# Hybrid decoder step on one core: another VectorE order while h is made, and norm2 written in place

## The chip, the core and the metric

The kernel runs on one core of a Trainium2 chip. A core has five engines that run their own instruction streams and meet through semaphores: TensorE (PE) multiplies matrices, VectorE (DVE) and ScalarE (ACT) do elementwise work, GpSimd (POOL) and SyncE (SP) issue transfers here. The metric is the time of one execution on the device in microseconds, the median of several.

## The reference, cut to what matters

One layer of a decoder trunk over 1056 tokens (1024 of a prompt, 32 of samples: 8 requests of 4) with 1024 features:

```python
mod = (silu(c) @ w_ada + b_ada).reshape(bsz, 6, D_MODEL)      # shift1, scale1, gate1, shift2, scale2, gate2
h = rmsnorm(x, norm1_g) * (1 + scale1) + shift1
u_ssm, u_pool, g_ssm, g_pool = split(h @ w_in)                # 1024 -> 3072
y_ssm = s5_mixer(u_ssm, ...)                                  # diagonal complex state space model
merged = sigmoid(g_ssm) * glu(gelu(y_ssm)) + sigmoid(g_pool) * pool_mixer(u_pool, ...)
x = x + gate1 * (merged @ w_out)
h2 = rmsnorm(x, norm2_g) * (1 + scale2) + shift2
f_a, f_b = split(h2 @ w_ffn_in)
x = x + gate2 * ((silu(f_a) * f_b) @ w_ffn_out)
y = rmsnorm(x, normf_g)
```

The modulations differ between the prompt and each sample request. All inputs and outputs are float32.

## The kernel before

**Tiles.** Activations lie with features on the 128 partitions and tokens along the row: X[k], k = 0 to 7, is a tile of 128 features by 1056 tokens. Tokens go in three column groups G0 = 0 to 384, G1 = 384 to 768, G2 = 768 to 1056; the last 32 columns are the samples. Every float32 operand is kept as a high and a low part, and each product is three matmuls: high by high (L510), low activation by high weight (L511), high activation by low weight (L512). For an activation the high part is written by ACT and the low part by DVE; `split` (L484) makes the parts of a weight, `whi` on ACT (L488) and `wlo` on DVE (L489), in a ring of four buffers each.

**The start.** The sums of squares of x run through PE (L685), DVE takes the reciprocal root (`rsqrt`, L563 to L573), PE broadcasts it with four `pick` matmuls, and ACT copies them to R (L710, L711). In between come the modulations of feature tiles 0 and 1: `ada_main(m, hq)` multiplies w_ada on PE (L609) and copies the result with ACT to `adat` (L695); `ada_fin` turns it with two small matmuls (L616) and writes mod[m] on DVE (L619, L621, L623), m = 1 for the scale and m = 0 for the shift. hq counts pairs of feature tiles, so hq = 0 to 3.

**The h stage.** For each feature tile, `h_scale` scales x in place on DVE (L641, and three small operations for the samples, L598 to L600) and has ACT add the shift into `hh` (L644); `h_lo` makes `hl` on DVE from x, the shift and `hh` (L648). The first two column tiles of w_in, f = 0 and 1, are accumulated while the feature tiles appear: `gemm(kt, f)` multiplies feature tile kt. Between gemm(kt, 0) and gemm(kt, 1) of kt = 0, 2, 4 stand the modulations of the next pair.

**The S5 preparation.** The coefficients of the state space model are worked out by small DVE operations that are recorded first and written out later by `fill(n)`, n of them at a time (all have line L93); `fill(1000)` at the end of the h stage writes those that are left. Then S5 makes the matrices `wbr` and `wbi` (L125 to L131), which PE transposes into `tp` (L265), between pieces of the column tiles f = 2 and f = 3, each over all eight feature tiles.

**Norm 2 and the FFN.** After w_out, `residual` (L944) adds to X in place, and `norm2(g)` makes h2 for a column group: it scales X into a tile `xn` (L979), ACT and DVE make the high and low parts, and POOL stores `xn` to `hd` in HBM, and after the last group X to `xr` (L989). For the first FFN steps `ffn_in` (L1030) runs on h2; then `sums` loads pieces of `hd` back (`bq`, by SP, L1051), forms sums of them on DVE (`bf`, L1056 to L1059), and splits these (`th` on ACT, L1066; `tl` on DVE, L1067) for `product` (L1108), which runs the other FFN steps with fewer products of blocks (L1114 to L1116).

**What sets the order.** PE and SP keep the order in which the program is written, to the end. DVE and ACT keep it as long as `order` is open, which is until the column tile f = 3 is done; behind that a scheduler orders them by what is ready.

Of the kernel before, what the change touches and what calls it, by code (L numbers as in the profile page):

```python
# [10 lines left out]
F32 = mybir.dt.float32  # L11
# [16 lines left out]
NTOK = 1056  # L28
# [424 lines left out]
def trunk(ctx: ExitStack, tc: tile.TileContext, A, O):  # L453
    nc = tc.nc
# [37 lines left out]
    def split2(src):  # L492
        raw = load(src)
        return [split(raw[:, i]) for i in range(2)]

    def ahead(srcs):

        nxt = split2(srcs[0])
        for i in range(len(srcs)):
            cur, nxt = nxt, split2(srcs[i + 1]) if i + 1 < len(srcs) else None  # L500
            yield cur
# [132 lines left out]
    s5c = third.enter_context(pool("s5c"))  # L634
    s5 = S5(tc, s5c, psum, dram, ident, A["s5"], yd, O["pst"], O["sst"])

    wgen = ahead([A["w_in"][i] for i in (*range(2, 16), 22, 23, *range(16, 22))] + [A["w_glu"][i] for i in range(8)] + [A["w_out"][0]])

    def h_scale(kt, a=0, b=NTOK):
        x, e = X[kt], min(b, ST)  # L640
        v.scalar_tensor_tensor(x[:, a:e], x[:, a:e], mod[1][:, kt, 0:1], R[:, a:e], op0=MUL, op1=MUL)  # L641
        if b > ST:
            modulate_samples(x[:, ST:], R[:, ST:], mod[1], mod[0], kt, x[:, ST:])
        act.activation(hx(kt)[0][:, a:b], x[:, a:b], AF.Identity, bias=mod[0][:, kt, 0:1], scale=1.0)  # L644

    def h_lo(kt, a=0, b=NTOK):
# [5 lines left out]
    with ExitStack() as early:  # L652
        ring = early.enter_context(pool("ada"))
        s5t = early.enter_context(pool("s5t"))
        raw = {}

        def fetch(hq):
            for m in (1, 0):
                raw[m, hq] = [load(A["w_ada"][m, hq, pg], ring) for pg in range(2)]

        fetch(0)
        us_raw = [load(A["w_in"][f]) for f in range(2)]
        fetch(1)
        fetch(2)
        v.tensor_reduce(r32, ident.rearrange("p (q t) -> p t q", q=4), axis=mybir.AxisListType.X, op=ADD)
        prep = s5.prep(s5t)
        next(prep)
        for _ in prep:
            pass
        fill = s5.later.emit  # L670
        fetch(3)
        sq = (page("sq"), page("R1"))
        R = sq[1]
        ss = mm((128, 264))
        for k in range(8):
            q = sq[k % 2]
            for h in range(2):
                qh, xh = (z[:, 528 * h:528 * h + 528] for z in (q, X[k]))
                if h and k in (3, 5, 7):
                    v.tensor_mul(qh, xh, xh)  # L680
                    fill(5)
                else:
                    act.activation(qh, xh, AF.Square)
                for r in (2 * h, 2 * h + 1):
                    pe.matmul(ss[32 * r:32 * r + 32, :], ones[:, 0:32], q[:, 264 * r:264 * r + 264], start=k == 0,  # L685
                              stop=k == 7, tile_position=(0, 32 * r))
        act.activation(prm[:, 0:256], prm[:, 0:256], AF.Silu)
# [12 lines left out]

        x, y, t = (tmp()[:, 0:264] for _ in range(3))
        rsqrt(ss, x, y, t)
        ada_main(1, 0)
        ada_main(0, 0)
        ada_fin(0)
        fill(4)
        us_w = [[split(us_raw[f][:, 0])] for f in range(2)]
        for r in range(4):
            ps = mm((128, 264))
            pe.matmul(ps, pick[:, r, :], y, start=True, stop=True)  # L710
            act.copy(R[:, 264 * r:264 * r + 264], ps)  # L711
        us_ps = [[mmg(g) for g in range(3)] for f in range(2)]

        def gemm(kt, f):
            for g in range(3):
                feat(us_ps[f][g], w8(us_w[f]), hx, g, [kt], kt == 0, kt == 7)

        def ada_pair(hq):
            for m in (1, 0):
                ada_main(m, hq)  # L720

        h_scale(0, *GROUPS[0])
        h_scale(0, *GROUPS[1])
        h_lo(0, *GROUPS[0])
        h_scale(0, *GROUPS[2])
        h_lo(0, *GROUPS[1])
        h_scale(1)
        h_lo(0, *GROUPS[2])
        for kt in range(8):
            gemm(kt, 0)  # L730
            if kt < 6 and kt % 2 == 0:
                ada_pair(kt // 2 + 1)
            gemm(kt, 1)
            if kt < 6:
                if kt % 2 == 0:
                    ada_fin(kt // 2 + 1)
                h_scale(kt + 2)
            if kt < 7:
                h_lo(kt + 1)
            if kt == 1:  # L740
# [6 lines left out]
    s5.pool = s5p  # L747
    pump = Pump(s5.run())

    w_next = next(wgen)  # L750
    for f in range(4):
        if f >= 2:
            w = w_next if f == 2 else next(wgen)
        if f == 2:
            pumps.append(pump)
        for g in range(3):
            if f < 2:
                ps = us_ps[f][g]
# [201 lines left out]
    acc, R = page("acc2"), page("R2")  # L960
    mx = h2x = hx
    xr = dram.tile([8, 128, NTOK], F32, name="xr")
    hd = dram.tile([8, 128, NTOK], F32, name="hd")
    md = dram.tile([22, 128, 2, NTOK], F32R, name="md")

    def norm2(g):
        a, b = GROUPS[g]
        e = min(b, ST)
        stores = []
        yield 3.0  # L970
        for us in rstd(acc, g, R, 5.0):
            yield us if isinstance(us, float) else 1.0
        for k in range(8):
            hi, lo = h2x(k)
            sc, sh = mod[4][:, k, 0:1], mod[3][:, k, 0:1]
            n = e - a
            t = quart("xn") if g == 2 else pE.tile([128, 384], F32, name="xn", tag="xn", bufs=4)
            t = t[:, 0:b - a]
            v.scalar_tensor_tensor(t[:, 0:n], X[k][:, a:e], sc, R[:, a:e], op0=MUL, op1=MUL)  # L979
            if b > ST:  # L980
                modulate_samples(X[k][:, e:b], R[:, e:b], mod[4], mod[3], k, t[:, n:])
            act.activation(hi[:, a:b], t, AF.Identity, bias=sh, scale=1.0)
            v.scalar_tensor_tensor(lo[:, a:b], t, sh, fp(hi[:, a:b]), op0=ADD, op1=SUB)
            stores.append((hd[k, :, a:b], t))
            if g == 2:
                stores.append((xr[k], X[k]))
            if k % 2:
                for s in stores:
                    gp.dma_start(*s)  # L989
                stores.clear()  # L990
            yield 1.0

    with pool("pE") as pE:
        dsh = prm[:, 0:4]
        v.tensor_sub(dsh, mod[3][:, 0:4, 0], mod[3][:, 4:8, 0])
        wo = [next(wgen)]
        for d in range(1, 8):
            raw = load(A["w_out"][d])
            wo.append([split(raw[:, i], pE, "wo", 14) for i in range(2)])
        for g in range(3):  # L1000
            if g == 2:
                fw = [split2(A[n][0]) for n in ("w_ffn_a", "w_ffn_b")]
# [331 lines left out]
```

## Time and profile before

| | us |
|---|---|
| three runs, median | 1364.84 |
| lowest and highest | 1362.89 to 1368.11 |
| the profiled execution | 1364.88 |
| its span, first to last instruction | 1362.9 |

| engine | busy us | share of the span | instructions |
|---|---|---|---|
| PE | 1306.8 | 96% | 9248 |
| DVE | 778.0 | 57% | 1805 |
| ACT | 420.2 | 31% | 801 |
| POOL | 149.9 | 11% | 297 |

Matmuls are counted apart from the weight loads that overlap them. The chain of work that ended last is 91% PE. A timeline row gives the start and the busy time of an instruction or of a run of like ones, and in brackets how long the engine stood idle before it and what released it.

### The profile page before, as it was taken

The page shows a single profiled execution, that of the slowest core. Times are in us where ns is not written, and L with a number is a line of the kernel's source. Part 1 is how long each engine was busy: PE and PEld are TensorE (multiplying, and loading weights), DVE is VectorE, ACT ScalarE, POOL GpSimd, SP SyncE. Part 2 cuts the span into 40 slices and gives each one's busy share as a digit, 9 for nine tenths or more (in the row PEclk, how much of TensorE's full clock was granted, in tenths as well). Part 3 has the DMA queues.
Part 4 walks back from the last instruction along what each step waited for, and adds up shares of the span by engine and source line. Part 5 has one row for each costly group of instructions (what it writes and reads, how often), then busy time and mean ns, then how long its engine had stood idle before and what let it go on. Part 6 is the DMA issues. An engine that isn't in the chain of part 4 may idle for free.

```text
span 1362.9 us, 23083 instructions
## 1 busy us (share of the span) xinstructions
PE 1306.8 (96%) x9248; PEld 1255.2 (92%) x9248; DVE 778.0 (57%) x1805; ACT 420.2 (31%) x801; POOL 149.9 (11%) x297
## 2 busy tenths in 40 slices
PE   6779999999999999999799999999999999999995
PEld 2679999999898999999799999999999999999995
DVE  6586986744214556556866566666566433333357
ACT  5222442233722324223433333333333211111121
POOL 0002121112000000112101001001001331000000
PEclk8879999999999999999999999999999999999998
DMA  9223042133544544226533333333333793424203
GB/s 382 91 83 109 10 124 58 59 99 89 173 139 140 185 166 141 76 88 224 155 92 111 96 109 112 94 111 111 92 114 111 238 399 134 168 86 139 70 1 128
DMA packets 73211, 173.95 MB, mean 128 GB/s; under 512 B 9808, under 2 KB 26384, under 8 KB 73104
## 3 DMA queue, kind: packets, MB, share of 16 engines
q1 hardware_dynamic: 42816, 97.12, 22.4%
q0 software_dynamic: 27840, 72.52, 15.9%
q10 hardware_dynamic: 2448, 2.84, 0.7%
q8 instruction: 72, 1.18, 0.4%
q14 instruction: 35, 0.29, 0.1%
HBM read 130.17 MB, written 42.27 MB: 127 GB/s over the span
## 4 chain that ended last, share of the span: by engine, by line
PE 91%; DVE 6%; DMA 2%; issue 1%; SPq 0%; ACT 0%; DVEq 0%; ACTq 0%
PE mm L510 19%; PE mm L512 18%; PE mm L511 18%; PE b L1115 10%; PE b L1116 10%; PE b L1114 10%; PE aux L609 2%; DMA raw<-in_w_ada 1%; PE yp L381 1%; PE vp L320 1%; PE aux L616 1%; PE yp L377 1%; DVE hl L648 1%; DVE tl L1067 1%; DVE xf L1249 1%
## 5 line engine op out<-in xcount | busy, mean ns | idle before, releaser
L511 PE MATMUL mm<-hl,whi 128*128 128x384 f32 (+1 forms) x864 | 283.0, 328 | 11.4 <-DVE hl L648 11.4
L510 PE MATMUL mm<-hh,whi 128*128 128x384 f32 (+1 forms) x864 | 288.5, 334 | 1.9 <-ACT hh L644 1.0
L512 PE MATMUL mm<-hh,wlo 128*128 128x384 f32 (+1 forms) x864 | 282.6, 327 | 7.6 <-DVE wlo L489 7.6
L1114 PE MATMUL b<-th,whi 128*128 128x264 f32 x640 | 183.2, 286 | 4.4 <-ACT th L1066 4.4
L1115 PE MATMUL b<-tl,whi 128*128 128x264 f32 x640 | 183.2, 286 | 3.3 <-DVE tl L1067 3.3
L1116 PE MATMUL b<-th,wlo 128*128 128x264 f32 x640 | 182.8, 286 | 0.0
L510 PEld LDWEIGHTS mm<-hh,whi 128*128 128x128 f32 x864 | 165.1, 191 | 15.8 <-issue 11.6
L511 PEld LDWEIGHTS mm<-hl,whi 128*128 128x128 f32 x864 | 165.3, 191 | 13.1 <-DVE hl L648 13.1
L512 PEld LDWEIGHTS mm<-hh,wlo 128*128 128x128 f32 x864 | 165.2, 191 | 7.9 <-DVE wlo L489 7.9
L510 PE MATMUL mm<-mh,whi 128*128 128x352 f32 (+3 forms) x528 | 171.0, 324 | 0.0
L512 PE MATMUL mm<-mh,wlo 128*128 128x352 f32 (+3 forms) x528 | 170.6, 323 | 0.0
L511 PE MATMUL mm<-ml,whi 128*128 128x352 f32 (+3 forms) x528 | 170.5, 323 | 0.0
L489 DVE TENSOR_TENSOR wlo<-raw,whi 128x512 fp32r<-128x512 f32 (+1 forms) x144 | 89.7, 643 | 138.2 <-ACT whi L488 137.6
L488 ACT CAST whi<-raw 128x512 fp32r<-128x512 f32 (+1 forms) x144 | 81.2, 584 | 230.2 <-PE mm L511 194.3
L1115 PE MATMUL b<-hl,whi 128*128 128x264 f32 x480 | 136.5, 284 | 0.0
L1116 PE MATMUL b<-hh,wlo 128*128 128x264 f32 x480 | 136.2, 284 | 0.0
L1114 PE MATMUL b<-hh,whi 128*128 128x264 f32 x480 | 136.1, 284 | 0.0
L1114 PEld LDWEIGHTS b<-th,whi 128*128 128x128 f32 x640 | 121.2, 189 | 4.6 <-ACT th L1066 4.6
L1115 PEld LDWEIGHTS b<-tl,whi 128*128 128x128 f32 x640 | 121.0, 189 | 3.8 <-DVE tl L1067 3.8
L1116 PEld LDWEIGHTS b<-th,wlo 128*128 128x128 f32 x640 | 121.1, 189 | 0.0
L510 PEld LDWEIGHTS mm<-mh,whi 128*128 128x128 f32 x528 | 99.4, 188 | 0.9 <-issue 0.2
L512 PEld LDWEIGHTS mm<-mh,wlo 128*128 128x128 f32 x528 | 99.5, 188 | 0.5
(339 smaller groups left out, 2156.6 us busy)
## 6 DMA issues: line engine op xcount, KB each, us to landing
raw<-in_w_ada SPq DMA_DIRECT2D x64, 256.0 KB, 3.1
raw<-in_w_in SPq DMA_DIRECT2D x24, 512.0 KB, 4.2
mh<-md POOLq DMA_DIRECT2D x22, 528.0 KB, 8.2
ml<-md POOLq DMA_DIRECT2D x22, 528.0 KB, 9.1
raw<-in_w_ffn_a SPq DMA_DIRECT2D x22, 512.0 KB, 3.5
raw<-in_w_ffn_b SPq DMA_DIRECT2D x22, 512.0 KB, 3.6
md<-mh POOLq DMA_DIRECT2D x40, 264.0 KB, 2.3
md<-ml POOLq DMA_DIRECT2D x40, 264.0 KB, 2.6
```

What stands on the lines that cost most here:

```text
L320: nc.tensor.matmul(vp[64 * g:64 * g + 64, ri, 0:136], wt[:, ri, i, 64 * g:64 * g + 64], U[:, 2 * i + g, 8:144], start=True, stop=True, til ...
L377: nc.tensor.matmul(yps[h][:, k, :], mt[:, 2 * i + h, :], U[:, 2 * i + h, 0:136], start=True, stop=False)
L381: nc.tensor.matmul(yps[h][:, k, :], V[ri][R, i, 1:9, :], S[ri][R, i, 0:136], start=False, stop=ri == 1)
L488: act.copy(hi, raw)
L489: v.tensor_sub(lo, raw, fp(hi))
L510: pe.matmul(ps, wh, xh[:, a:b], start=first and kt == kts[0], stop=False)
L511: pe.matmul(ps, wh, xl[:, a:b], start=False, stop=False)
L512: pe.matmul(ps, wl, xh[:, a:b], start=False, stop=last and kt == kts[-1])
L609: pe.matmul(ps[32 * r:32 * r + 32, :], sil[:, kt, :], w[:, o:o + 256], start=kt < 4, stop=kt >= 4, tile_position=(0, 32 * r))
L1114: pe.matmul(o, wh, xh, start=first and k == 0, stop=False, skip_group_check=True)
L1115: pe.matmul(o, wh, xl, start=False, stop=False, skip_group_check=True)
L1116: pe.matmul(o, wl, xh, start=False, stop=k == 3, skip_group_check=True)
```

## The change

**While h is made.** `h_scale` is cut into `h_t` (DVE) and `h_hi` (ACT), and the loop over kt is written out with another order. The modulations of hq = 0 are cut: mod[1] is finished ahead of the broadcasts, mod[0]'s matmuls come between the second and the third broadcast. The first halves of the weights of f = 0 and 1 are split behind the first `hh`, not ahead of R. The modulations of hq = 1 come between the column groups of gemm(0, 0), and `hl1` ahead of them on DVE; likewise `hl3` ahead of mod of hq = 2. The weights of f = 2 are split ahead of `fill(1000)` and those of f = 3 behind it; before, both stood behind it. The counts of `fill` at the start change from 5, 5, 5 and 4 to 4, 4, 6 and 5.

**Norm 2.** It scales X in place, `xn` and `hd` are gone with their 24 stores, and `sums` reads X where it loaded 16 pieces `bq`. Since X is overwritten, X is stored to `xr` for each feature tile and column group right behind its residual and square: 24 stores of a third of the size in place of 8.

```diff
-    def h_scale(kt, a=0, b=NTOK):
+    def h_t(kt, a=0, b=NTOK):
         x, e = X[kt], min(b, ST)
         v.scalar_tensor_tensor(x[:, a:e], x[:, a:e], mod[1][:, kt, 0:1], R[:, a:e], op0=MUL, op1=MUL)
         if b > ST:
             modulate_samples(x[:, ST:], R[:, ST:], mod[1], mod[0], kt, x[:, ST:])
+
+    def h_hi(kt, a=0, b=NTOK):
+        x = X[kt]
         act.activation(hx(kt)[0][:, a:b], x[:, a:b], AF.Identity, bias=mod[0][:, kt, 0:1], scale=1.0)
...
                     v.tensor_mul(qh, xh, xh)
-                    fill(5)
+                    fill(4 if k < 7 else 6)
...
         ada_main(1, 0)
-        ada_main(0, 0)
-        ada_fin(0)
-        fill(4)
-        us_w = [[split(us_raw[f][:, 0])] for f in range(2)]
+        ada_fin(0, (1,))
+        fill(5)
         for r in range(4):
...
+            if r == 1:
+                ada_main(0, 0)
+        h_t(0, *GROUPS[0])
+        ada_fin(0, (0,))
+        h_hi(0, *GROUPS[0])
+        h_t(0, *GROUPS[1])
+        h_hi(0, *GROUPS[1])
+        us_w = [[split(us_raw[0][:, 0])]]
+        h_lo(0, *GROUPS[0])
+        h_t(0, *GROUPS[2])
+        h_hi(0, *GROUPS[2])
+        h_lo(0, *GROUPS[1])
+        us_w.append([split(us_raw[1][:, 0])])
+        h_t(1)
+        h_hi(1)
+        h_lo(0, *GROUPS[2])
...
-        def gemm(kt, f):
+        def gemm(kt, f, between=()):
             for g in range(3):
                 feat(us_ps[f][g], w8(us_w[f]), hx, g, [kt], kt == 0, kt == 7)
+                if g < len(between):
+                    ada_main(*between[g])
...
-        for kt in range(8):
-            gemm(kt, 0)
-            if kt < 6 and kt % 2 == 0:
-                ada_pair(kt // 2 + 1)
-            gemm(kt, 1)
-            if kt < 6:
-                if kt % 2 == 0:
-                    ada_fin(kt // 2 + 1)
-                h_scale(kt + 2)
-            if kt < 7:
-                h_lo(kt + 1)
-            if kt == 1:
-                for f in range(2):
-                    us_w[f].append(split(us_raw[f][:, 1]))
+        gemm(0, 0, ((1, 1), (0, 1)))
+        h_lo(1)
+        gemm(0, 1)
+        ada_fin(1)
+        h_th(2)
+        h_th(3)
+        h_lo(2)
+        gemms(1)
+        ada_pair(2)
+        gemm(2, 0)
+        h_lo(3)
+        ada_fin(2)
+        h_th(4)
+        for f in range(2):
+            us_w[f].append(split(us_raw[f][:, 1]))
+        h_th(5)
+        h_lo(4)
+        gemm(2, 1)
+        gemms(3, lambda: ada_pair(3))
+        ada_fin(3)
+        h_th(6)
+        h_lo(5)
+        h_th(7)
+        h_lo(6)
+        gemms(4)
+        h_lo(7)
+        for kt in range(5, 8):
+            gemms(kt)
+        us_w.append(split2(A["w_in"][2]))
         fill(1000)
...
     def norm2(g):
...
-            t = quart("xn") if g == 2 else pE.tile([128, 384], F32, name="xn", tag="xn", bufs=4)
-            t = t[:, 0:b - a]
-            v.scalar_tensor_tensor(t[:, 0:n], X[k][:, a:e], sc, R[:, a:e], op0=MUL, op1=MUL)
+            t = X[k][:, a:b]
+            v.scalar_tensor_tensor(t[:, 0:n], t[:, 0:n], sc, R[:, a:e], op0=MUL, op1=MUL)
...
-            stores.append((hd[k, :, a:b], t))
-            if g == 2:
-                stores.append((xr[k], X[k]))
...
                 square(X[d], g, acc, d == 0)
+                a, b = GROUPS[g]
+                gp.dma_start(xr[d][:, a:b], X[d][:, a:b])
...
-            q = [quart("bq") for _ in range(4)]
-            for i, z in enumerate(q):
-                nc.sync.dma_start(z, hd[k + 4 * (i // 2), :, 528 * (i % 2):528 * (i % 2) + 528])
-            b11, b12, b21, b22 = q
+            b11, b12, b21, b22 = (X[k + 4 * i][:, 528 * j:528 * j + 528] for i in range(2) for j in range(2))
```

In the lists below, the line numbers of the changed kernel differ a little from those of the kernel before.

What stands in a row on ACT at the start, before (`adat` the two modulations of hq = 0, `whi` the two first weight halves, `R1` the copies of R, `hh0` and `hh1` the high parts of h):

```order
L695 COPY adat_361<-aux_352 128x256
L695 COPY adat_372<-aux_363 128x256
L488 CAST whi_388<-raw_150 128x512
L488 CAST whi_392<-raw_152 128x512
L711 COPY R1_261<-mm_396 128x264
L711 COPY R1_261<-mm_399 128x264
L711 COPY R1_261<-mm_402 128x264
L711 COPY R1_261<-mm_405 128x264
L644 ACTIVATE hh0_112<-x0_82,mod0_107 128x384 x2
```

and after:

```order
L695 COPY adat_360<-aux_351 128x256
L709 COPY R1_261<-mm_372 128x264
L709 COPY R1_261<-mm_375 128x264
L695 COPY adat_387<-aux_378 128x256
L709 COPY R1_261<-mm_389 128x264
L709 COPY R1_261<-mm_392 128x264
L644 ACTIVATE hh0_112<-x0_82,mod0_107 128x384 x2
L488 CAST whi_404<-raw_150 128x512
L644 ACTIVATE hh0_112<-x0_82,mod0_107 128x288
L488 CAST whi_415<-raw_152 128x512
```

The two `whi` moved behind the first two groups of `hh0`; the second `adat` moved between the copies of R.

On DVE in the h stage, where mod of hq = 1 is written (`x2`, `x3` the feature tiles 2 and 3 scaled in place, `hl1`, `hl2` low parts), before:

```order
L619 TENSOR_TENSOR mod0_107<-aux_476,prm_81 128x18
L623 TENSOR_TENSOR mod0_107<-mod0_107 128x2x8
L641 SCALAR_TENSOR_TENSOR x2_86<-x2_86,mod1_106,R1_261 128x1024
L598 TENSOR_TENSOR x2_86<-x2_86,R1_261 128x32
L599 TENSOR_TENSOR x2_86<-x2_86,mod1_106 128x32
L600 TENSOR_TENSOR x2_86<-x2_86,mod0_107 128x32
L648 SCALAR_TENSOR_TENSOR hl1_115<-x1_84,mod0_107,hh1_114 128x1056
L641 SCALAR_TENSOR_TENSOR x3_88<-x3_88,mod1_106,R1_261 128x1024
L598 TENSOR_TENSOR x3_88<-x3_88,R1_261 128x32
L599 TENSOR_TENSOR x3_88<-x3_88,mod1_106 128x32
L600 TENSOR_TENSOR x3_88<-x3_88,mod0_107 128x32
L648 SCALAR_TENSOR_TENSOR hl2_117<-x2_86,mod0_107,hh2_116 128x1056
```

and after:

```order
L648 SCALAR_TENSOR_TENSOR hl1_115<-x1_84,mod0_107,hh1_114 128x1056
L618 TENSOR_TENSOR mod1_106<-aux_472,prm_81 128x18
L620 SCALAR_TENSOR_TENSOR mod1_106<-mod1_106,prm_81 128x18
L618 TENSOR_TENSOR mod0_107<-aux_477,prm_81 128x18
L622 TENSOR_TENSOR mod0_107<-mod0_107 128x2x8
L638 SCALAR_TENSOR_TENSOR x2_86<-x2_86,mod1_106,R1_261 128x1024
L597 TENSOR_TENSOR x2_86<-x2_86,R1_261 128x32
L598 TENSOR_TENSOR x2_86<-x2_86,mod1_106 128x32
L599 TENSOR_TENSOR x2_86<-x2_86,mod0_107 128x32
L638 SCALAR_TENSOR_TENSOR x3_88<-x3_88,mod1_106,R1_261 128x1024
L597 TENSOR_TENSOR x3_88<-x3_88,R1_261 128x32
L598 TENSOR_TENSOR x3_88<-x3_88,mod1_106 128x32
```

`hl1` moved from behind mod and x2 to ahead of mod, and nothing of another tile stands now between x2 and x3; `hl2` still follows the end of x3.

On DVE where the sums of h2 start (`sa` and `ml` end an FFN step, `bf` are the sums, `tl` their low parts), before:

```order
L1056 SCALAR_TENSOR_TENSOR bf_6642<-bq_6633,prm_81,bq_6635 128x528
L1057 SCALAR_TENSOR_TENSOR bf_6640<-bf_6642,mod3_110,bq_6632 128x528
L1058 TENSOR_TENSOR bf_6641<-bq_6632,bq_6633 128x528
L1059 SCALAR_TENSOR_TENSOR bf_6643<-bf_6640,mod3_110,bq_6634 128x528
L1038 TENSOR_TENSOR sa_6733<-sa_6733,mm_6628 128x384
L1067 TENSOR_TENSOR tl_6649<-bf_6640,th_6648 128x528
L1067 TENSOR_TENSOR tl_6649<-bf_6641,th_6648 128x528
```

and after:

```order
L1081 SCALAR_TENSOR_TENSOR bf_6601<-xr0_5375,prm_81,xr4_5383 128x528
L1082 SCALAR_TENSOR_TENSOR bf_6599<-bf_6601,mod3_110,xr0_5375 128x528
L1083 TENSOR_TENSOR bf_6600<-xr0_5375 128x528
L1084 SCALAR_TENSOR_TENSOR bf_6602<-bf_6599,mod3_110,xr4_5383 128x528
L1081 SCALAR_TENSOR_TENSOR bf_6657<-xr1_5377,prm_81,xr5_5385 128x528
L1092 TENSOR_TENSOR tl_6608<-bf_6599,th_6607 128x528
L1092 TENSOR_TENSOR tl_6608<-bf_6600,th_6607 128x528
L1082 SCALAR_TENSOR_TENSOR bf_6655<-bf_6657,mod3_110,xr1_5377 128x528
L1083 TENSOR_TENSOR bf_6656<-xr1_5377 128x528
L1092 TENSOR_TENSOR tl_6614<-bf_6601,th_6613 128x528
```

The `bf` read `xr0`, `xr1`, `xr4`, `xr5` (X) in place of `bq`, and rows of the next k moved ahead of the `sa` that was next.

## Rows read from the trace of the kernel before

**Rows 1.** The page: busy tenths of PE in 40 equal slices.

```profile
PE   6779999999999999999799999999999999999995
```

**Rows 2.** Waits of PE: line, engine waited for, us in total, times, longest.

```profile
PE mm L511 <- DVE hl L648: 11.4, 6, 3.2
PE mm L512 <- DVE wlo L489: 7.6, 1, 7.6
...
PE b L1114 <- ACT th L1066: 4.4, 1, 4.4
PE b L1115 <- DVE tl L1067: 3.3, 2, 1.9
```

**Rows 3.** Windows of PE: stretch, us, busy (x), granted clock, DMA share, GB/s.

```profile
42.20:45.50 3.30, 3.30 (x14) 0.50 0.00 0
88.10:93.40 5.30, 5.30 (x17) 0.50 0.80 246
136.00:300.00 164.00, 162.60 (x1118) 1.00 0.23 66
```

**Rows 4.** Timeline of DVE, end of the reciprocal root: start us, us, instruction.

```profile
19.80 0.51 DVE L573 SCALAR_TENSOR_TENSOR tmp<-tmp 128x132 f32<-128x132 f32 x2
```

**Rows 5.** Timeline of PE, start and h stage.

```profile
21.72 3.71 PE L710 MATMUL mm<-tmp,pick 128*128 128x264 f32 x8
...
31.50 3.64 PE L609 MATMUL aux<-raw,prm 128*32 128x256 f32 x32
...
36.77 0.95 PE L616 MATMUL aux<-r,adat 128*128 128x9 f32 x8
...
47.08 1.93 PE L609 MATMUL aux<-raw,prm 128*32 128x256 f32 x32
```

**Rows 6.** Timeline of ACT in the h stage.

```profile
25.74 1.12 ACT L644 ACTIVATE hh<-x,mod 128x384 fp32r<-128x384 f32 x2
...
39.93 1.18 ACT L644 ACTIVATE hh<-x,mod 128x1056 fp32r<-128x1056 f32 x1 [4.29 <-DVE x L600]
```

**Rows 7.** Timeline of DVE, feature tiles 2 and 3.

```profile
37.31 0.18 DVE L619 TENSOR_TENSOR mod<-aux,prm 128x18 f32<-128x18 f32 x1 [6.64 <-PE aux L616]
...
38.06 1.28 DVE L641 SCALAR_TENSOR_TENSOR x<-x,mod,R 128x1024 f32<-128x1024 f32 x1
...
39.81 1.31 DVE L648 SCALAR_TENSOR_TENSOR hl<-x,mod,hh 128x1056 fp32r<-128x1056 f32 x1
41.04 1.28 DVE L641 SCALAR_TENSOR_TENSOR x<-x,mod,R 128x1024 f32<-128x1024 f32 x1
```

**Rows 8.** Timeline of DVE around the S5 preparation.

```profile
72.81 0.22 DVE L93 TENSOR_SCALAR f_b<-f_r 128x128 f32<-128x128 f32 x1
...
87.36 2.48 DVE L489 TENSOR_TENSOR wlo<-raw,whi 128x512 fp32r<-128x512 f32 x4
...
93.20 0.69 DVE L131 TENSOR_TENSOR wbi<-t,t 128x512 f32<-128x512 f32 x1
```

**Rows 9.** Timeline of PE, first transposes and first matmul of f = 3.

```profile
97.08 0.60 PE L265 MATMUL tp<-ident,wbr 128*128 128x128 f32 x4
...
102.73 0.34 PE L510 MATMUL mm<-hh,whi 128*128 128x384 f32 x1
```

**Rows 10.** Timeline of DVE at the first sums.

```profile
648.89 0.76 DVE L1056 SCALAR_TENSOR_TENSOR bf<-bq,prm 128x528 f32<-128x528 f32 x1
...
655.33 0.56 DVE L1038 TENSOR_TENSOR sa<-sa,mm 128x384 f32<-128x384 f32 x1 [3.58 <-PE mm L512]
```

**Rows 11.** Timeline of PE, its last wait for a sum.

```profile
680.64 0.59 PE L1115 MATMUL b<-tl,whi 128*128 128x264 f32 x1 [1.89 <-DVE tl L1067]
```

**Rows 12.** DMA issues: x count, KB each, median us to landing.

```profile
xr<-xr POOLq DMA_DIRECT2D x8, 528.0 KB, 3.6
```

**Rows 13.** Timeline of POOL, the last store of X.

```profile
621.34 0.53 POOL L989 DMA_DIRECT2D xr<-xr  x1 [2.59 <-DVE xr L953]
```

**Rows 14.** Timeline of DVE, norm 2 of the last group.

```profile
630.98 0.49 DVE L979 SCALAR_TENSOR_TENSOR xn<-xr,mod,R 128x256 f32<-128x256 f32 x1
```

More of the change, by code (lines that the diff above doesn't have):

```diff
@@ L494, in split2, with ahead @@
         return [split(raw[:, i]) for i in range(2)]
-    def ahead(srcs):
-        nxt = split2(srcs[0])
+    def ahead(srcs, nxt):
         for i in range(len(srcs)):
@@ L635, in trunk @@
     s5 = S5(tc, s5c, psum, dram, ident, A["s5"], yd, O["pst"], O["sst"])
-    wgen = ahead([A["w_in"][i] for i in (*range(2, 16), 22, 23, *range(16, 22))] + [A["w_glu"][i] for i in range(8)] + [A["w_out"][0]])
-    def h_scale(kt, a=0, b=NTOK):
+    def h_t(kt, a=0, b=NTOK):
         x, e = X[kt], min(b, ST)
@@ L711, in trunk, with gemms, h_th @@
             act.copy(R[:, 264 * r:264 * r + 264], ps)
+            if r == 1:
[14 more added lines that the diff above has]
+        h_lo(0, *GROUPS[2])
         us_ps = [[mmg(g) for g in range(3)] for f in range(2)]
-        def gemm(kt, f):
+        def gemm(kt, f, between=()):
             for g in range(3):
                 feat(us_ps[f][g], w8(us_w[f]), hx, g, [kt], kt == 0, kt == 7)
+                if g < len(between):
+                    ada_main(*between[g])
+        def gemms(kt, then=None):
+            gemm(kt, 0)
+            if then:
+                then()
+            gemm(kt, 1)
+        def h_th(kt):
+            h_t(kt)
+            h_hi(kt)
         def ada_pair(hq):
@@ L720, in ada_pair @@
                 ada_main(m, hq)
[L722 to L728, printed above, removed]
-        for kt in range(8):
-            gemm(kt, 0)
-            if kt < 6 and kt % 2 == 0:
-                ada_pair(kt // 2 + 1)
-            gemm(kt, 1)
-            if kt < 6:
-                if kt % 2 == 0:
-                    ada_fin(kt // 2 + 1)
-                h_scale(kt + 2)
-            if kt < 7:
-                h_lo(kt + 1)
-            if kt == 1:
-                for f in range(2):
-                    us_w[f].append(split(us_raw[f][:, 1]))
+        gemm(0, 0, ((1, 1), (0, 1)))
[27 more added lines that the diff above has]
+        us_w.append(split2(A["w_in"][2]))
         fill(1000)
@@ L748, in trunk @@
     pump = Pump(s5.run())
-    w_next = next(wgen)
     for f in range(4):
-        if f >= 2:
-            w = w_next if f == 2 else next(wgen)
         if f == 2:
+            w = us_w[2]
+            wgen = ahead([A["w_in"][i] for i in (*range(3, 16), 22, 23, *range(16, 22))]
+                         + [A["w_glu"][i] for i in range(8)] + [A["w_out"][0]], split2(A["w_in"][3]))
             pumps.append(pump)
+        elif f == 3:
+            w = next(wgen)
         for g in range(3):
@@ L962, in trunk @@
     xr = dram.tile([8, 128, NTOK], F32, name="xr")
-    hd = dram.tile([8, 128, NTOK], F32, name="hd")
     md = dram.tile([22, 128, 2, NTOK], F32R, name="md")
@@ L968, in norm2 @@
         e = min(b, ST)
-        stores = []
         yield 3.0
@@ L976, in norm2 @@
             n = e - a
-            t = quart("xn") if g == 2 else pE.tile([128, 384], F32, name="xn", tag="xn", bufs=4)
-            t = t[:, 0:b - a]
-            v.scalar_tensor_tensor(t[:, 0:n], X[k][:, a:e], sc, R[:, a:e], op0=MUL, op1=MUL)
+            t = X[k][:, a:b]
+            v.scalar_tensor_tensor(t[:, 0:n], t[:, 0:n], sc, R[:, a:e], op0=MUL, op1=MUL)
             if b > ST:
-                modulate_samples(X[k][:, e:b], R[:, e:b], mod[4], mod[3], k, t[:, n:])
+                modulate_samples(t[:, n:], R[:, e:b], mod[4], mod[3], k, t[:, n:])
             act.activation(hi[:, a:b], t, AF.Identity, bias=sh, scale=1.0)
             v.scalar_tensor_tensor(lo[:, a:b], t, sh, fp(hi[:, a:b]), op0=ADD, op1=SUB)
-            stores.append((hd[k, :, a:b], t))
-            if g == 2:
-                stores.append((xr[k], X[k]))
[L987 to L990, printed above, removed]
             yield 1.0
```

## The prediction

> **What bounds the kernel now.** The table of engines comes first: PE is busy for 1306.8 us of a span of 1362.9, so all that any change of order can win is the 56 us in which PE stands. The page's slices of PE [rows 1] say where these lie: slices 1 to 3 (each 34 us long), slice 20 and the last; all others read 9. So the change is looked at where it touches the first three slices, which is the h stage, and near 650 us, where the sums of h2 are made. The waits of PE [rows 2] name what ended last in both: for the h stage 11.4 us in six waits for `hl` and 7.6 us in one wait for `wlo`, for the sums 4.4 us on `th` and 3.3 us on `tl`. Between 136 and 300 us PE is busy for 162.6 of 164 us [rows 3]: time won before it is not lost there by waiting, it moves all that follows. In the h stage no engine is full: DVE waits for a modulation that stands behind PE (6.64 us idle ahead of L619 [rows 7]), and PE then waits for DVE. That ring of waits is what the new order cuts.
>
> **Part 1, the h stage, walked through in the new order.** Start: `rsqrt` ends at 20.3 [rows 4]. Four broadcasts take 3.71 us, the 16 matmuls of one `ada_main` 1.82 (half of 3.64) and the first L616 result 0.54 (36.77 to L619 at 37.31), so mod[0] begins at 26.4 [rows 5, 7]. A pair of mods takes 0.75 (37.31 to 38.06 [rows 7]), one half of it, so it is there at 26.75; ACT then makes two `hh` (1.12 [rows 6]) and, only now, the first `whi` (I take 0.62, a quarter of 2.48 for the four `wlo` [rows 8]): PE begins at 28.6. From there PE has 9 matmuls at half clock, 0.31 each (5.30 us for 17 [rows 3]), 32 of `ada_main` at 3.64 [rows 5] and 9 at twice the clock, 2.8 + 3.64 + 1.4, and 0.8 of waits for the low parts of tile 0: gemm(0, 1) ends at 37.2. L616 and the mods make x2 begin at 38.5, against 38.06 [rows 7]. So the start loses 0.4 us.
>
> From here DVE sets the pace. A tile costs it 1.75 us for x (38.06 to 39.81) and 1.23 for `hl` (39.81 to 41.04) [rows 7]. hl1 is already done, which PE before waited for behind mod and x2. x2, x3, hl2 end at 43.2; hl3 waits for its `hh` (1.18 on ACT [rows 6]) and ends at 44.65. PE meanwhile runs gemms(1) and the next `ada_main` pair (1.93 at full clock [rows 5]), then gemm(2, 0), and mod for tiles 4 and 5 is ready at 46.1. x4 ends at 47.85. Then the new order has DVE wait: the two `wlo` need `whi`, which stands on ACT behind hh4; 1.9 us pass until 49.75. With two `wlo` (1.24), x5 and hl4, DVE is at 53.95. The ACT copies of the third pair of modulations stand behind hh5, so its mod begins at 55.0 and x6 at 55.75. x6, hl5, x7, hl6, hl7 (7.2 of DVE work, and 0.15 for a last `hh`) end at 63.1, two `wlo` of f = 2 at 64.35, and `fill(1000)` begins there, against 72.81 [rows 8]. The gain on DVE is 8.46 us.
>
> **Part 2, from fill to f = 3.** The fill keeps its instructions and its 14.55 us (72.81 to 87.36); from its end to the end of `wbi` it was 6.53 (to 93.89), now without two `wlo`, 5.29 [rows 8]. So `wbi` is there at 84.2. PE before stood 7.6 us for the first `wlo` of f = 2 and then ran into the transposes at 97.08 without waiting [rows 2, 9]. Now it has `wlo` early: its own h products end near 67, the 39 matmuls of f = 2 ahead of the transposes take 6.8, and at 74 it waits 10 us for `wbi`. From the transposes to the first matmul of f = 3 it needs 5.65 us at full clock (97.08 to 102.73 [rows 9]).
>
> The clock. Behind a wait of 7.6 us, PE ran at a granted clock of 0.50, which is 1.2 GHz, for 5.30 us (88.10 to 93.40), and behind a wait of 3.2 us for 3.30 us [rows 2, 3]. The new 10 us wait is nearest to the first, so half of 5.30, 2.65 us, is added (half of 3.30, 1.65, is the lower bound, and 4.0 the upper, if the slow stretch grows with the wait). f = 3 begins at 84.2 + 5.65 + 2.65 = 92.5, which against 102.73 is **10.2 us** earlier (8.8 to 11.2).
> The Trainium skill, in "TensorE: Matmul & The Clock Gate", section "HAM oscillation — how this bites in real kernels", says that a long idle gap throws the array back to half clock and that the restart is paid again at every such gap. The trace agrees, twice [rows 3], and this speaks against a change that gathers short waits into one long one: by the rule the gain here is 10.2, without it 12.9 and the time 1348.6.
>
> What is late next: DVE's S5 work behind the transposes is in its queue before PE gets there, and the weights of the next column tiles wait for buffers that PE itself frees, so these move along. SP loses nothing here; it keeps its loads.
>
> **Part 3, norm 2 and the sums.** Removed are 24 POOL stores and 16 SP loads, none of which PE waits for [rows 2]. DVE keeps its instructions. What changes is when `bf` may begin: it needs no load, so the scheduler has put the second group's `bf` and `tl` ahead of the `sa` for which DVE stood 3.58 us at 655.33 [rows 10]. From 648.89 to the last `tl` that PE waited for, which ended about 680.6 [rows 10, 11], that is DVE's only idle time, so all `tl` come up to 3.58 earlier; I take **3.4**, since an instruction seldom ends just with the gap. PE's waits there add up to 7.7 us [rows 2], so they can pay it. Bounds: 0, if the later `sa` holds PE's banks, and 3.6.
> The added cost: 24 shorter stores in place of 8. X may be overwritten when its store has landed. The last one before was issued at 621.34 and lands in about 3.6 us; the last group is scaled from 630.98 on [rows 12 to 14]. Margin: some 6 us for the first tile, whose store stands seven tiles earlier still. Taken at nothing; the price without this cover is the third rival.
>
> **Sum.** 10.2 + 3.4 = 13.6 us off the profiled execution, 1364.88, which is the median of the runs (1364.84) to 0.04: **1351.3**. About 2 us of it lie outside the span and stay.
>
> **Rivals.**
> *Handoffs slip (smaller gain).* Each of the three modulations passes PE, ACT, PE, DVE, and the walk gives them no slack. If each costs 1 to 1.5 us more than in the rows, the fill starts 4 us later, and all of it reaches the transposes, since PE waits for DVE there: 1355.3. For it: the new order puts two things behind `hh` on ACT. Against: the same handoffs are in the durations that I took from 36.77 to 38.06.
> *The stage gives nothing.* If DVE was not what set its end, because ACT's `hh` or PE's half clock do, the fill starts about when it did, and the sums alone are left: 1364.88 − 3.4 = 1361.5. Against: DVE stands idle for 6.64 us in one place [rows 7], which is not work of ACT. The case that the gain is lost again in the S5 stage ends at the same time.
> *Larger gain.* PE's restart is not on the path (12.9), and PE's waits at the sums vanish to 5 us: 1364.88 − 12.9 − 5 = 1347.
> *Slower: the write in place waits for the store.* DVE keeps its order, so an L979 that waits for POOL's store holds the residuals, `sa` and `bf` queued behind it, and PE waits for these. With one landing of 3.6 us nothing is late. It begins to cost from a landing of 9.6 us (621.34 to 630.98 [rows 13, 14]), and the kernel is slower than before only if a landing passes 9.6 + 13.6 = 23 us; at 33 us, it takes about 1374. Against: 3.6 us for three times the size [rows 12].
> The Trainium skill, in "SBUF — State Buffer", section "🔬 SBUF: two separate sides", says that a transfer issued from POOL can starve while certain VectorE operations run, because its descriptors can't be written. No row here shows a store that starved so; the rule is the reason why this rival is not at nought.
>
> **How the numbers follow.** Forecast 1351.3, own range 1348 to 1354.5 (clock 1 us either way, sums 0 to 3.6, handoffs 1 to 2): 0.66. Slipped handoffs, about 1355: 0.14. Larger gain, about 1347: 0.08. Nothing from the stage, 1361.5: 0.08. Slower, about 1374: 0.04. A measurement of this kernel tells about 0.5% from no change, 6.8 us, so faster means below 1358.0: the first three, 0.88; the fourth is within it, 0.08; the last 0.04. The range takes in the forecast, most of the slipped handoffs and half of the larger gain: 1346.0 to 1357.5, with 2 in 10 outside.
>
> **What the profile after would show.** Right: the wait of PE for `wlo` (7.6) gone, and one of about 10 us for `wbi` or `wbr` at L265 in its place; `f_b`, the first row of the fill, near 64; f = 3 from about 92.5; a granted clock of 0.50 behind the transposes; the waits for `hl` well under 11.4; no idle 3.58 at the first `sa`, and the waits for `th` and `tl` down by 3.4 together. Wrong: `f_b` behind 68 (handoffs), the transposes early and f = 3 late (clock), or DVE waits for a store at norm 2 (the slower case).

## The result, and the profile after

The changed kernel takes 1351.5 us in the median of three runs (1350.71 to 1352.82), against 1365.84 for the kernel before beside it: a ratio of 0.990, with a 95% interval of 0.987 to 0.9925. A fourth run was disturbed (3229.7 us) and is left out; with it the median is 1352.16, the number from which the expectations below start. The forecast was 1351.3. The profiled execution took 1352.82 with a span of 1351.0, against 1364.88 and 1362.9: 11.9 us less of span, where the sum had 13.6.

The waits of PE in the changed kernel (line, engine waited for, us in total, times, longest):

```profile
PE tp L265 <- DVE wbr L127: 6.8, 1, 6.8
...
PE b L1140 <- DVE tl L1092: 2.4, 1, 2.4
...
PE tp L265 <- DVE wbi L131: 2.0, 2, 1.0
...
PE b L1139 <- ACT th L1091: 1.7, 1, 1.7
PE mm L510 <- DVE hl L648: 0.8, 1, 0.8
```

Beside [rows 2]: the 11.4 us of waits for `hl` are 0.8, the 7.6 us for `wlo` are gone, waits of 6.8 and 0.9 us stand ahead of the transposes instead, and the waits for `tl` and `th` fell from 7.7 to 4.1 us.

DVE in the changed kernel, from the end of `rsqrt` to `wbi` (start us, us, instruction, idle before and its releaser):

```profile
20.42 0.50 DVE L572 SCALAR_TENSOR_TENSOR tmp<-tmp 128x132 f32<-128x132 f32 x2
...
40.15 1.28 DVE L638 SCALAR_TENSOR_TENSOR x<-x,mod,R 128x1024 f32<-128x1024 f32 x1
...
51.27 1.29 DVE L489 TENSOR_TENSOR wlo<-raw,whi 128x512 fp32r<-128x512 f32 x2 [1.75 <-ACT whi L488]
...
56.49 0.18 DVE L618 TENSOR_TENSOR mod<-aux,prm 128x18 f32<-128x18 f32 x1 [0.94 <-PE aux L615]
...
65.74 0.23 DVE L93 TENSOR_SCALAR f_b<-f_r 128x128 f32<-128x128 f32 x1
...
85.06 0.69 DVE L131 TENSOR_TENSOR wbi<-t,t 128x512 f32<-128x512 f32 x1
```

Beside [rows 4, 7, 8]: x2 begins at 40.15, not 38.06, but the last fill begins at 65.74, not 72.81, and `wbi` ends 8.1 us earlier.

PE in the same stretch, its first matmul on h, the transposes and the first matmul of f = 3, and three windows (stretch, us, busy, granted clock, DMA share, GB/s):

```profile
29.56 0.45 PE L509 MATMUL mm<-hh,whi 128*128 128x384 f32 x1 [2.16 <-ACT whi L488]
...
83.75 1.11 PE L265 MATMUL tp<-ident,wbr 128*128 128x128 f32 x4 [6.80 <-DVE wbr L127]
85.81 1.11 PE L265 MATMUL tp<-ident,wbi 128*128 128x128 f32 x4 [0.94 <-DVE wbi L131]
...
93.74 0.34 PE L509 MATMUL mm<-hh,whi 128*128 128x384 f32 x1
```

```profile
20.50:24.00 3.50, 2.94 (x16) 0.50 1.03 417
24.00:27.00 3.00, 3.00 (x18) 0.52 1.03 410
```

```profile
86.00:91.50 5.50, 5.50 (x21) 0.50 0.47 59
```

f = 3 begins at 93.74, not 102.73 [rows 9], 9.0 us earlier. Behind the new wait PE runs 5.5 us at half clock; so it does for 6 us at the start, behind the wait for `rsqrt`.

At the first sums DVE no longer stands 3.58 us before an `sa` [rows 10]:

```profile
638.54 0.76 DVE L1081 SCALAR_TENSOR_TENSOR bf<-xr,prm,xr 128x528 f32<-128x528 f32 x1
...
646.39 0.76 DVE L1084 SCALAR_TENSOR_TENSOR bf<-bf,mod,xr 128x528 f32<-128x528 f32 x1
647.07 0.55 DVE L1066 TENSOR_TENSOR sa<-sa,mm 128x384 f32<-128x384 f32 x1
```

The stores of X are shorter, and the last is issued long before X is written again (DMA issues, then POOL, then DVE):

```profile
xr<-xr POOLq DMA_DIRECT2D x16, 192.0 KB, 2.2
xr<-xr POOLq DMA_DIRECT2D x8, 144.0 KB, 2.0
```

```profile
611.33 0.54 POOL L1035 DMA_DIRECT2D xr<-xr  x1 [2.39 <-DVE xr L989]
```

```profile
624.57 0.48 DVE L1012 SCALAR_TENSOR_TENSOR xr<-xr,mod,R 128x256 f32<-128x256 f32 x1
```

That is tile 7, whose store was the last: 13.2 us between issue and overwriting, for a landing of 2.

### The profile page after: what moved, and what is told of

Its sections match the earlier page's. It is cut to its first block, busy times and chain, and to the rows that moved or that the text cites. A ratio compares the mean times of both kernels' runs of the same rounds, so it can differ in the third digit from the quotient of the medians.

```text
span 1351.0 us, 23011 instructions
## 1 busy us (share of the span) xinstructions
PE 1307.0 (97%) x9248; PEld 1254.5 (93%) x9248; DVE 777.9 (58%) x1805; ACT 419.0 (31%) x801; POOL 146.2 (11%) x289
## 4 chain that ended last, share of the span: by engine, by line
PE 91%; DVE 7%; issue 1%; DMA 1%; ACT 0%; SPq 0%; DVEq 0%; ACTq 0%
PE mm L509 19%; PE mm L510 18%; PE mm L511 18%; PE b L1140 10%; PE b L1141 10%; PE b L1139 10%; PE aux L608 2%; PE yp L381 1%; PE vp L320 1%; PE yp L377 1%; PE aux L615 1%; DVE xf L1274 1%; DVE wlo L489 0%; PE aux L588 0%; DVE tl L1092 0%
```

## The experiments

Two numbers of each profile are used below: where f = 3 begins, and what is left of the span behind that point. The first tells of the h stage (and of the start, which differs by up to 1.6 us between executions of the same instructions, as the last experiment shows), the second of norm 2 and the sums. Each ratio is to runs of the kernel before taken beside that kernel.

| kernel | median us | ratio to before, 95% | f = 3 begins | span | rest of span |
|---|---|---|---|---|---|
| before | 1364.8 to 1365.8 | 1 | 102.73 | 1362.9 | 1260.2 |
| changed | 1351.5 | 0.987 to 0.9925 | 93.74 | 1351.0 | 1257.3 |
| h stage only | 1356.13 | 0.9925 to 0.995 | 92.70 | 1353.4 | 1260.7 |
| norm 2 only | 1359.96 | 0.996 to 0.998 | 101.27 | 1357.3 | 1256.0 |
| `wlo` ahead only | 1364.1 | 0.998 to 1.000 | 101.81 | 1362.3 | 1260.5 |
| PE kept running | 1349.68 | 0.987 to 0.990 | 91.11 | 1348.4 | 1257.3 |
| low parts behind | 1355.5 | 0.992 to 0.994 | 97.97 | 1354.6 | 1256.6 |
| ACT earlier | 1349.43 | 0.987 to 0.990 | 90.40 | 1348.0 | 1257.6 |
| fill spread | 1344.92 | 0.984 to 0.987 | 84.73 | 1341.2 | 1256.5 |
| ring of 7 | 1351.71 | 0.989 to 0.992 | 91.23 | 1349.1 | 1257.9 |
| spread, `wlo` late | 1341.6 | 0.982 to 0.985 | 81.81 | 1339.4 | 1257.6 |
| all | 1340.25 | 0.981 to 0.984 | 79.96 | 1336.9 | 1256.9 |
| PE kept at the start | 1350.76 | 0.988 to 0.991 | 91.21 | 1349.8 | 1258.6 |

The intervals of kernels within some 3 us of each other overlap, so between those the rows decide.

**The two parts apart.** The first takes the diff without its edits to `norm2` and `sums`, the second those alone.

> The new order of the h stage alone; norm 2 and the sums as before. Theory (the two parts add up, and each acts only where it stands): f = 3 begins at about 93.7 us as in the changed kernel, against 102.7 before, and nothing is given back, so 9.0 us less than before: 1356.8 for a median of before of 1365.8. PE still waits 7.7 us for th and tl at the sums. Rival (the whole gain comes from the h stage, the sums gave nothing): 1352.5. Rival (part of the 9 us is given back later): 1360 or more.

> Norm 2 in place and the sums read from X alone; the h stage as before. Theory: the waits for th and tl fall from 7.7 to about 4.1 us, 3.6 us less than before, 1362.2. The writes in place wait for no store. Rival (the sums' gain is borrowed from elsewhere, say from the earlier start of the stage): 1365.8, no change.

Measured: 1356.13, 8.7 us below its 1364.85, and 1359.96, 4.9 below (interval 2.7 to 5.9, which holds the 3.6 expected). Together 13.6, where both at once gave 14.3 by the medians and 14.0 by the ratio. The rest of the span is 1260.2 to 1260.7 us wherever norm 2 is as before, and 1256.0 to 1258.6 wherever it is changed: about 3.2 us in the mean, near the 3.6 that PE's waits for `th` and `tl` lost. With the h stage alone these waits are 4.4 and 3.3 us as before, and with norm 2 alone they are:

```profile
PE b L1104 <- DVE tl L1056: 2.4, 1, 2.4
...
PE b L1103 <- ACT th L1055: 1.6, 1, 1.6
```

4.0 us in place of 7.7. So the parts add up within the intervals, and neither gain is borrowed from the other.

**The wait for `wlo` taken away alone**, in the kernel before:

```diff
+        us_w.append(split2(A["w_in"][2]))
         fill(1000)
...
+            w = us_w[2]
+            wgen = ahead([A["w_in"][i] for i in (*range(3, 16), ...)] + ..., split2(A["w_in"][3]))
```

> The kernel before with one edit: the weights of f = 2 are split ahead of the last fill, those of f = 3 behind it. Theory: PE's 7.6 us wait for wlo goes, but wbi ends at 93.9 as before, since DVE does the same work up to there; PE waits for the transposes, then runs at half clock, and f = 3 begins at about 102.2 instead of 102.7: 0.5 us less, 1365.3. Rival (the wait named in the table of waits is what is lost): 7.6 us less, 1358.2.

```profile
PE tp L265 <- DVE wbr L127: 6.2, 1, 6.2
...
PE tp L265 <- DVE wbi L131: 1.9, 2, 1.0
```

Measured 1364.1, 0.7 below before, ratio 0.998 to 1.000: hardly told apart from no change, while 7.6 us less is excluded. In the waits of PE the longest wait of the S5 stage, 7.6 us, vanished, and 6.2 and 0.9 us stand at the transposes. `wbi` ends at 93.74, before at 93.89. The row in the table of waits was not the price: DVE's chain up to `wbi` was.

**The slow clock behind the long wait.** In the changed kernel, 36 matmuls into the transposes' bank, whose result is overwritten:

```diff
             tp = s.psum.tile([128, 512], F32, name="tp", tag="aux", bufs=2)
+            if q == 0 and ri == 0:
+                s.warm(tp)
...
+            def warm(tp):
+                for _ in range(36):
+                    pe.matmul(tp[:, 0:384], us_w[2][1][0][:, 0:128], hx(0)[0][:, 0:384], start=True, stop=True)
```

> The changed kernel with 36 extra matmuls of 384 columns into the transposes' own bank just ahead of the first transpose, some 6.3 us of work in the 6.8 us in which PE waits there; their result is overwritten. Theory (half the slow stretch behind that wait, 5.5 us at a granted clock of 0.50, is a loss of about 2.7): the clock stays at 1.00 behind the transposes, f = 3 begins at about 91.0 instead of 93.7, and the time is 2.7 us lower than the changed kernel's 1352.2: 1349.5. Rival (DVE's work behind the transposes sets the pace, so the clock costs nothing): 1352.2.

The extra work and the transposes behind it, and the window from there to f = 3:

```profile
76.86 6.41 PE L792 MATMUL tp<-hh,whi 128*128 128x384 f32 x36
83.80 0.66 PE L267 MATMUL tp<-ident,wbr 128*128 128x128 f32 x4 [0.54 <-DVE wbr L127]
```

```profile
83.70:91.10 7.40, 5.90 (x41) 1.00 0.72 141
```

`wbr` comes no earlier (83.80 against 83.75), and PE's first matmul on h came at 29.52, as at 29.56, yet f = 3 begins at 91.11, 2.6 us earlier, and the span is 2.6 us shorter. The medians, 1349.68 and 1351.5, differ by 1.8, with intervals that overlap, so the size rests on the profiles. The restart, put at 2.65 in the prediction, costs just that in this pair of executions; in the seven profiles with a wait of 6.2 to 7.7 us there, PE took 9.3 to 10.1 us from the first transpose to f = 3, against 7.3 here, so it costs 2.0 to 2.8. The Trainium skill, in "TensorE: Matmul & The Clock Gate", section "HAM oscillation — how this bites in real kernels", says that the restart is paid again at each long gap; the trace agrees, with 2.6 us for this one.

**The low parts put back behind the next modulation:**

```diff
         gemm(0, 0, ((1, 1), (0, 1)))
-        h_lo(1)
         gemm(0, 1)
         ada_fin(1)
         h_th(2)
+        h_lo(1)
         h_th(3)
...
-        h_lo(3)
         ada_fin(2)
         h_th(4)
+        h_lo(3)
```

> The changed kernel, with hl1 put back behind mod of hq = 1 and x2, and hl3 behind mod of hq = 2 and x4, all else as changed. Theory (a low part behind the next modulation makes PE wait for it, and the modulation after that comes later by the same amount): each costs about 3 us, so the last fill starts near 71 us and not 65.7, f = 3 at about 99, and the time is some 5.5 us above the changed kernel: 1357.7. Rival (what counts is the split of the modulations between the column groups, not the low parts): 1352.2.

```profile
PE mm L510 <- DVE hl L648: 5.8, 4, 3.2
```

```profile
27.91 0.69 PE L509 MATMUL mm<-hh,whi 128*128 128x384 f32 x1 [2.16 <-ACT whi L488]
```

```profile
69.92 0.22 DVE L93 TENSOR_SCALAR f_b<-f_r 128x128 f32<-128x128 f32 x1
```

PE waits 5.8 us for `hl` again, and the fill begins at 69.92. This execution began its h stage 1.65 us earlier than that of the changed kernel (27.91 against 29.56, with the same code up to there), so from the first matmul on h to the fill it took 42.0 us, against 36.2: 5.8 more, as expected. The medians differ by only 4.0, the ratios by 0.003 (4.2 us) with intervals that overlap a little. That the low parts count is shown by the two rows and the wait; their size lies between 4.0 and 5.8. f = 3 still begins 4.8 us earlier here than in the kernel before (97.97 against 102.73); which of the other moves gives that, no run takes apart, beyond the 0.9 us of `wlo` alone.

**ACT's casts and copies earlier** (`cast` is the part of `split` on ACT, `rest` that on DVE):

```diff
+        half = [cast(us_raw[f][:, 1]) for f in range(2)]
         ada_fin(2)
         h_th(4)
         for f in range(2):
-            us_w[f].append(split(us_raw[f][:, 1]))
-        h_th(5)
+            us_w[f].append(rest(*half[f]))
+        h_t(5)
...
         gemms(3, lambda: ada_pair(3))
+        h_hi(5)
```

> The changed kernel, with the casts of the second weight halves ahead of hh4 on ACT, and the copies of the last pair of modulations ahead of hh5. Theory (the 1.75 us in which DVE waits for whi behind x4, and about 0.9 us ahead of the last mod, lie on the path): the last fill starts 2.6 us earlier, f = 3 at about 91.1, 1349.6. Rival (other waits of DVE take their place, since PE sets the pace there): 1352.2.

DVE at the two `wlo`, at the last mod and at the fill:

```profile
49.02 1.29 DVE L499 TENSOR_TENSOR wlo<-raw,whi 128x512 fp32r<-128x512 f32 x2
...
53.82 0.18 DVE L628 TENSOR_TENSOR mod<-aux,prm 128x18 f32<-128x18 f32 x1 [0.54 <-PE aux L625]
...
63.07 0.22 DVE L93 TENSOR_SCALAR f_b<-f_r 128x128 f32<-128x128 f32 x1
```

Measured 1349.43, 2.1 below the changed kernel, with intervals that overlap; the fill begins 33.7 us behind the first matmul on h (29.35 to 63.07), not 36.2. Of the two handoffs that the prediction had found at 49.75 and 55.0, the wait of 1.75 us is gone and that of 0.94 is 0.54, so both were on the path; this run moves them together, and how much each gave alone is not shown.

**The fill in DVE's waits.** `fill(n)` is put ahead of the places at which DVE stands, for example:

```diff
         h_t(0, *GROUPS[0])
+        fill(12)
         ada_fin(0, (0,))
```

> The changed kernel, with 40 operations of the last fill moved into the places of the h stage at which DVE waits (3, 12, 4, 2, 3, 5, 2, 6 and 3 of them); the others stay. Theory (DVE's work up to wbi is the path, and its waits in the h stage are free time): wbi ends near 77 and not 85.7, PE reaches the transposes at about 76.8 and hardly waits, so it keeps its clock, f = 3 begins at about 83 and not 93.7, and the time is about 10.5 us lower, 1341.5. Rival (the pieces push the modulations back by as much as they save): 1352. Rival (gained here, given back behind it, where weights come no earlier): between 1345 and 1352.

DVE and PE at the end of the stage:

```profile
74.14 1.29 DVE L489 TENSOR_TENSOR wlo<-raw,whi 128x512 fp32r<-128x512 f32 x2 [2.65 <-ACT whi L488]
...
78.73 0.69 DVE L131 TENSOR_TENSOR wbi<-t,t 128x512 f32<-128x512 f32 x1
```

```profile
77.42 0.66 PE L265 MATMUL tp<-ident,wbr 128*128 128x128 f32 x4 [1.18 <-DVE wbr L127]
```

1344.92, 6.6 us below the changed kernel; f = 3 begins 9.0 earlier in the profile, and the rest of the span, 1256.5, gives nothing back, though the median lies at the edge of the last rival's range. The profiled executions differ by 9.8 us (1352.82, the slowest of its three, and 1343.01, the fastest of its four), so the gain lies between 6.6 and 9.8. Of what is missing from 10.5, 1.7 us shows at f = 3 (84.73, not 83), behind a new wait: DVE now comes to the `wlo` of f = 3 before ACT has its `whi`. ACT casts it behind the copies of `u`, which stood for a store of `u`:

```profile
72.28 1.14 ACT L294 COPY u<-mm 128x384 f32<-128x384 f32 x3 [3.72 <-DMA ud<-u]
...
73.44 1.18 ACT L488 CAST whi<-raw 128x512 fp32r<-128x512 f32 x2
```

The next expectation puts this wait down to a buffer that PE frees; these rows name the store. Two versions follow from the wait, the weights of f = 3 split behind `wbi`, and this with ACT's order as above:

```diff
-            wgen = ahead(..., split2(A["w_in"][3]))
...
                 feat(ps, w8(w), hx, g, range(8))
+            if (f, g) == (2, 1):
+                wgen = ahead(..., split2(A["w_in"][3]))
```

> As the kernel with 40 operations of the fill spread (1344.9), and the weights of f = 3 split behind wbi, not ahead of it. There DVE stood 2.65 us for the whi of f = 3, which waits on ACT for PE to free a buffer. Theory (that wait took back part of the gain): wbi ends at about 76.8 and not 79.4, f = 3 begins at about 82.4 and not 84.7, 1342.6. Rival (the wlo of f = 3 comes too late now and PE waits for it): 1344.9 or more.

> The same with the casts and copies on ACT earlier as in the second experiment on them, and 31 operations of the fill spread, since two of the waits are gone. Theory (DVE up to wbi is the path, so the gains add): wbi at about 74.5, f = 3 at about 80.1, 1340.3. Rival (PE is the bound by now, since it reaches the transposes when wbi does): 1342.6.

```profile
76.17 0.60 PE L265 MATMUL tp<-ident,wbr 128*128 128x128 f32 x4
```

```profile
72.97 0.60 PE L265 MATMUL tp<-ident,wbr 128*128 128x128 f32 x4
...
74.70 0.66 PE L265 MATMUL tp<-ident,wbi 128*128 128x128 f32 x4 [1.13 <-DVE wbi L131]
```

1341.6 and 1340.25. In the first `wbi` ends at 75.4, earlier than the 76.8 expected, since the `wlo` of f = 3 themselves (1.29 us) left DVE's chain with the wait; PE comes to `wbr` without a wait, so PE sets the pace there. With ACT's order both meet within 1.1 us. f = 3 begins at 81.81 and 79.96. The last version beats both kernels: 0.981 to 0.984 of the kernel before. The step between the two is 1.35 us by the medians, where 2.3 was expected; their intervals overlap.

**What let the sums start earlier.** One size in the changed kernel, `tag="Q", bufs=11` to `bufs=7`:

> The changed kernel with 7 in place of 11 buffers in the ring from which the sums bf, the parts of the FFN's middle and, in the kernel before, the loaded pieces bq come. In the kernel before, bq held up to 4 of the 11. Theory (the sums start earlier since nothing has to be loaded): PE's waits for th and tl stay at about 4.1 us, whatever the later FFN steps lose by the smaller ring. Rival (they start earlier since four buffers came free): the waits go back to about 7.7 us, and DVE stands some 3 us before an sa or a bf again.

```profile
PE b L1140 <- DVE tl L1092: 2.4, 1, 2.4
...
PE b L1139 <- ACT th L1091: 1.7, 1, 1.7
```

The waits stay at 4.1, and the median is 1351.71, beside 1351.5. So four more buffers for `bf` were not what let them start earlier. That leaves the loads as what held `bf`, by exclusion; no run takes only them away. The ring had its part in them: in the kernel before, the last three loads of the second group were issued only at 652.08, when the last `bf` of the first group (651.00 to 651.76) was done with its `bq`:

```profile
652.08 1.29 SPq L1051 DMA_DIRECT2D bq<-hd  x3
```

**The start.** Six matmuls of `pick` by x in the bank of the first broadcast, overwritten by it:

```diff
             ps = mm((128, 264))
+            if r == 0:
+                for _ in range(6):
+                    pe.matmul(ps, pick[:, 0, :], X[0][:, 0:264], start=True, stop=True)
             pe.matmul(ps, pick[:, r, :], y, start=True, stop=True)
```

> The changed kernel with 6 extra matmuls (pick by x) ahead of the first broadcast, into its own bank, where PE waits 2.5 us for rsqrt; their result is overwritten. In the changed kernel PE ran the broadcasts and the modulation behind that wait at a granted clock of 0.50 for 6 us, which is on the path to the first mod. Theory (the wait let the clock fall): the clock is up at the broadcasts, PE's first matmul of h comes about 2.5 us earlier, and all behind it: 1349.7. Rival (the clock is down there for another reason and stays down, or the extra work itself delays the broadcasts): 1352.2 or more.

```profile
18.91 2.92 PE L710 MATMUL mm<-x,pick 128*128 128x264 f32 x12
21.66 1.05 PE L711 MATMUL mm<-tmp,pick 128*128 128x264 f32 x4
22.65 1.07 PE L608 MATMUL aux<-raw,prm 128*32 128x256 f32 x16
23.65 1.16 PE L711 MATMUL mm<-tmp,pick 128*128 128x264 f32 x4
...
27.31 0.44 PE L509 MATMUL mm<-hh,whi 128*128 128x384 f32 x1 [2.16 <-ACT whi L488]
```

The broadcasts take 1.05 and 1.16 us, where they took 2.10 each. They begin at 21.66, 0.7 us behind the end of `rsqrt` at 20.97, since the extra work lasts until then; PE's first matmul on h comes at 27.31, 2.25 us earlier than in the changed kernel's profile. The median is only 0.7 lower (1350.76), and the intervals overlap, so no gain in time is shown. A reason is seen in the other profiles: with the same code at the start, that matmul came at 29.35 to 29.56 in four executions (changed, PE kept running, h stage only, ACT earlier), but at 27.98 and 27.91 in two (ring of 7, low parts behind). Part of this is when the broadcasts begin (20.60 to 22.05), part the clock: from there to the first matmul on h these six took 7.30 to 8.69 us, and this one 5.65. Some executions raise the clock early without help.

## Why the prediction was right, step by step

*The start* was the worst step. The walk had mod[0] at 26.4 and PE at 28.6; they came at 27.4 and 29.56. `rsqrt` ended 0.6 later in this execution, and the broadcasts and the modulation between them, put at 3.71 + 1.82 = 5.5, took 6.1, at a clock of 0.50 to 0.52. The rest to x2, put at 9.9 (28.6 to 38.5), took 10.6. x2 is 1.65 late.

*The DVE walk* then held: x4 at 47.69 (46.1), the two `wlo` at 51.27 (49.75), x6 at 57.24 (55.75), the fill at 65.74 (64.35). The lag stays at 1.4 to 1.65 through 25 us, so the durations, the 1.9 us wait for `whi` and the late third modulation were sized right.

*From fill to f = 3.* `wbi` ends at 85.75 (84.2). PE waits 6.8 and 0.9, not 10: it came to the transposes at 76.95, not 74, as its h products ended at 70.1, not 67 (part of it is a stretch at half clock behind a wait of 2.0 us, which the walk did not have); this cost nothing, since it waited. The clock term, 2.65, was measured at 2.6; its upper bound, 4.0, follows from no row, as the two rows give 3.2 to 3.5 for a wait of 10 us. `wbi` is 1.55 late and f = 3 1.24, since the transposes of `wbr` had run by then, where the walk put all of them behind `wbi`. So f = 3 gained 9.0 us, not 10.2, and the difference is the start's.

*The sums*, put at 3.4, lost 3.6 us of waits, and 2.9 of span in the two profiled executions (3.2 over all of them). The reason, that `bf` needs no load, stood against the ring of buffers.

*The stores.* No instruction that writes X in place waits for one. The margin was greater than thought, as each store is issued right behind its residual.

*The rivals.* Handoffs that slip: the 1.65 us all lie ahead of x2, in the broadcasts and the first products, and none in the later modulations. Nothing from the stage, and slower: excluded. The larger gain was there to be had, but not by itself: keeping PE's clock gave 2.6 us of it.

The mechanism held term by term, but that the forecast of 1351.3 met the 1351.5 measured to 0.2 us is luck. The sum of 13.6 lies between the 11.9 by which the profiled executions differ (the start's 1.2 and the sums' 0.5 less) and the 14.3 of the medians, and the executions shown spread by 1.6 us in that start alone.

## What to carry to other kernels

A row in a table of waits names who came last, not what the wait is worth: the 7.6 us wait taken away alone gave 0.7 us, because DVE's chain up to `wbi`, for which PE then waited, ended no earlier. Walk the chain of the engine that is waited for, with the durations of the rows, through to the point where the other engine runs without a wait, and only then count. Where an engine that is on the path itself has waits, put its own later work into them: 40 small operations moved so gave another 6.6 us by the medians, on top of the 14.3 of the change.

## What the hardware showed that was not expected

On this path the clock of PE stood at 0.50 behind a wait of 2.5 us (ahead of the broadcasts) as behind one of 6.8 us (ahead of the transposes), and behind the second for 5.5 us. Behind a wait of 2.0 us (ahead of the last modulations, until 55.84) it stood at 1.00 for some 1.8 us more, and only then at 0.50:

```profile
55.80:57.50 1.70, 1.66 (x12) 1.00 0.37 149
57.70:60.90 3.20, 3.20 (x13) 0.50 0.00 0
```

How long it stays there varies from execution to execution with the same instructions: at the start, the first two broadcasts took 2.10 us and the last two 2.10 in the changed kernel's profile, but 2.10 and 1.16 with the ring of 7. From the first broadcast to the first matmul on h this is worth up to 1.4 us (7.30 to 8.69). Work that PE does for nothing, in a wait that it has anyway, was worth 2.6 us of span at the transposes.
